# Later modulation loads queued behind the weights that the text loads ahead of them

## The chip, the core and the metric

The kernel runs on one core of a Trainium2 chip. A core has a matmul engine (TensorE, PE in the profile; its weight loads are PEld), VectorE (DVE), ScalarE (ACT), GpSimd (POOL) and SyncE (SP), which here issues every DMA. The engines run their own instruction lists in order and meet at semaphores. The metric is the device time of one execution in microseconds (us).

## The reference, cut to what matters

Two layers of a diffusion backbone work on 512 latent tokens and 256 context tokens of width 2048, all in float32. Each layer first computes a modulation from a conditioning vector, then norm, one input projection, two kinds of attention heads, a gate, and one output projection:

```python
mod = silu_c @ w_mod[l] + b_mod[l]                 # (1, 3 * 2048), context: silu_cc
shift, scale, gate = jnp.split(mod[:, None, :], 3, axis=-1)
h = rmsnorm(x, norm_g[l]) * (1.0 + scale) + shift
u = h @ e_w_in[i]                                  # even layer; o_w_in in the odd one
...                                                # heads, SiLU gate
x = x + gate * (y @ w_o[l])
```

Layer 0 (even) has eight differential heads (A) and eight windowed heads (B), layer 1 (odd) eight heads with normalised q and k (C) and eight latent heads (D). Context is updated by layer 0 alone. A final RMSNorm follows.

## The kernel before, in words

**Where the weights go.** Activations are kept transposed, 16 tiles of 128 channels by 768 tokens. A projection (`proj`, L313) makes 128 output channels: it loads a column of weights in two loads of 512 KB (`wraw`, L298, three buffers), splits each into a high and a low part (`wsplit`: ScalarE makes `wh` at L289, VectorE `wl` at L248, four buffers each of four k tiles), and runs three matmuls per k tile and token group (L308, L309, L311). I call the weight loads w1, w2, ... in the order in which the text makes them: 8 at the start, 8 per head of heads 1 to 7 of A (w9 to w64), 40 in B (w65 to w104), 32 in the output projection (w105 to w136), then those of layer 1.

**Where the modulation goes.** Scale and shift of layer 0 come first, by TensorE (`mod_first`, L142; 88 loads at the very start). The rest, called the later modulation, is `mod_later` (L173): the gate of layer 0, then scale and shift of layer 1, then the gate of layer 1, in sixteen blocks of 512 columns. A block takes eight loads of 512 KB (`mraw`, two buffers, L180). Each load is multiplied by the conditioning value of its row and added up in `macc` (one buffer): two k rows times two vectors (latent and context), so four operations of VectorE per load (L187; ScalarE does the first two of a block, L185). The gate of layer 1 needs one vector, so two. After eight loads VectorE transposes `macc` into the last `mraw` (L196) and reduces it into `parts` (L197, one buffer); after four blocks a small matmul with `fold` (L204) into a bank of the projections' pool adds the partitions up, and VectorE writes `modc` (L210). The 128 loads are called M1 to M128.

**What sets their place.** `later` (L229) is a generator that makes one load with its arithmetic at each step. The text calls `tick(n)` at fixed points, which adds n to a due count and makes as many steps as have come due: 0.4 after each projection of heads 1 to 7 of A, 3.5 after most projections of B, 2 after each of the sixteen chunks of the output projection of layer 0 (capped at 96 until layer 1 starts), 3.5 twice per head of C. That is the order of the text only. A scheduler that plays a timeline of the program orders each engine's list: an instruction that is ready goes ahead of an earlier one of the text that has to wait. TensorE's list is written by hand only for the start (L418). A block `tc.issue_after(ins)` adds an ordering edge without a semaphore: every instruction made inside it on the engine of `ins` stands behind `ins` in that engine's list. Before the change the loads of M1 to M96 stand behind `last_raw`, the last load of the first modulation, and M97 to M128 behind `last_x`, the last load of layer 1's activations; so a weight load that waits for a free `wraw` buffer lets any number of later-modulation loads pass that find a free `mraw` buffer.

**Who needs the results.** The gate of layer 0 and the scale of layer 1 are read in `out_chunk` (L707), the shift of layer 1 in `make_h` (L375) at the start of layer 1, the gate of layer 1 in the last output projection.

Of the kernel before, what the change touches and what calls it, by code (L numbers as in the profile page):

```python
# [17 lines left out]
P = 128  # L18
# [23 lines left out]
def trunk_kernel(ctx: ExitStack, tc: tile.TileContext, T):  # L42
    nc = tc.nc
# [84 lines left out]
    def mod_scale(dst, g0, nk, nv):  # L128
        nc.vector.scalar_tensor_tensor(dst, dst, 1.0, vcol[:, g0:g0 + nk].unsqueeze(2).broadcast_to([P, nk, nv]),
                                       op0=ALU.add, op1=ALU.mult)  # L130
# [7 lines left out]
            mod_scale(dst, V_NG + 16 * l + k0 - NCH, nk, nv)  # L138

    last_raw = [None]  # L140

    def mod_first(g):  # L142

        acc = pst.tile([P, 512], F32, name="T")
        for r0 in range(0, 32, 3):
            n = min(3, 32 - r0)

            i = r0 // 3
            if i < (11, 11, 11, 11, 11, 6, 4, 3)[g]:
                raw = hslot("mraw0", F32)  # L150
            elif g == 7 and i > 8:
                raw = wp.tile([P, 1024], F32, name="mraw", bufs=2)
            else:
                raw = slot("mraw0")
            last_raw[0] = nc.sync.dma_start(raw[:, :n * 256], T["wm0"][g][:, r0 * 256:(r0 + n) * 256])
            for i in range(n):
                sec, at = divmod(r0 + i, NCH)
                j = at % 4
                nc.tensor.matmul(acc[32 * j:32 * j + 32, 256 * sec:256 * sec + 256], lhsT=sil[:, at, :],
                                 rhs=raw[:, 256 * i:256 * i + 256], start=(at < 4), stop=(at >= NCH - 4),  # L160
                                 tile_position=(0, 32 * j))
            if r0 + n < 32:
                yield
        asb = sp["ep"].tile([P, TOK], F32, name="e")[:, 0:512]
        nc.scalar.copy(asb, acc)
        yield
        for i in range(4):
            nc.tensor.matmul(acc[:, 2 * i:2 * i + 2], lhsT=asb[:, P * i:P * i + P], rhs=sel, start=True, stop=True)
        for sec in range(2):
            mod_finish(0, 2 * g + NCH * (1 - sec), 2, acc[:, 4 * sec:4 * sec + 4].rearrange("p (c v) -> p c v", c=2))  # L170
        yield

    def mod_later(l, b, nv, behind=None):  # L173

        macc = sm.tile([P, 2, 512], F32, name="macc", bufs=1)
        for r in range(8):
            raw = wp.tile([P, 1024], F32, name="mraw", bufs=2)
            rv = raw.rearrange("p (k c) -> p k c", k=2)
            with tc.issue_after(behind.ins) if behind is not None else nullcontext():
                nc.sync.dma_start(raw, T["wm1"][b + 4 if l else b - 8, r])  # L180
            for i in range(2):
                for v in range(nv):
                    sc = silc[:, 16 * v + 2 * r + i:16 * v + 2 * r + i + 1]
                    if r == 0 and i == 0:
                        nc.scalar.mul(macc[:, v, :], rv[:, i, :], sc)  # L185
                    else:
                        nc.vector.scalar_tensor_tensor(macc[:, v, :], rv[:, i, :], sc, macc[:, v, :],  # L187
                                                       op0=ALU.mult, op1=ALU.add)
            if r < 7:
                yield  # L190

        if b % 4 == 0:
            parts[0] = sm.tile([P, 128], F32, name="parts", bufs=1)[:, :64 * nv].rearrange("p (b v c) -> p b v c", b=4, v=nv)
        part = parts[0][:, b % 4, :, :]
        turned = raw.rearrange("p (v c) -> p v c", v=2)[:, 0:nv, :]
        nc.vector.transpose(turned, macc[:, 0:nv, :])  # L196
        nc.vector.reduce_sum(part, turned.rearrange("p v (b c) -> p v b c", c=32), axis=AX.X)  # L197
        if b % 4 < 3:
            yield
            return  # L200


        mp = psj.tile([P, 512], F32, name="J")
        nc.tensor.matmul(mp[:, 0:64 * nv], lhsT=fold, rhs=parts[0].rearrange("p b v c -> p (b v c)"), start=True, stop=True)  # L204
        mv = mp[:, 0:64 * nv].rearrange("p (b v a c) -> p b a v c", b=4, v=nv, c=4)
        k0 = 4 * b - 12
        for c in range(4):
            rows = slice(32 * c, 32 * c + 32)
            bias = bmod[rows, 48 * l + k0:48 * l + k0 + 16].rearrange("p (b a) -> p b a", b=4)
            nc.vector.tensor_tensor(modc[l][rows, k0:k0 + 16, 0:nv].rearrange("p (b a) v -> p b a v", b=4),  # L210
                                    mv[rows, :, :, :, c], bias.unsqueeze(3).broadcast_to([32, 4, 4, nv]), op=ALU.add)
        if k0 == NCH:
            mod_scale(modc[l][:, k0:k0 + 16, :], V_NG + 16 * l, 16, nv)
        yield
# [14 lines left out]
    def later():  # L229
        for b in range(8, 12):  # L230
            yield from mod_later(0, b, 2, last_raw[0])
        for b in (4, 5, 6, 7, 0, 1, 2, 3):
            yield from mod_later(1, b, 2, last_raw[0])
        for b in range(8, 12):
            yield from mod_later(1, b, 1, last_x)
# [58 lines left out]
    def wraw(w, col, k0, nk, raw=None):  # L294

        if raw is None:
            raw = wp.tile([P, 1024], F32, name="wraw", bufs=3)
        nc.sync.dma_start(raw[:, :nk * P], w[col // P][:, k0 * P:(k0 + nk) * P])  # L298
        return raw[:, :nk * P].rearrange("p (k c) -> p k c", k=nk)

    def mm_step(lat, cx, wk, xk, first, last, opens=True, closes=True, at=(0, 512)):
# [11 lines left out]
    def proj(w, col, xs=None, lat_only=False, at=(0, 512)):  # L313
        xs = hT if xs is None else xs
        n = len(xs)
        lat = psj.tile([P, 512], F32, name="J")[:, :at[1] - at[0]]
        cx = None if lat_only else psj.tile([P, 512], F32, name="J")[:, :256]
        for k0 in range(0, n, 8):
            nk = min(8, n - k0)
            ws = wsplit(wraw(w, col, k0, nk), nk)  # L320
            for i in range(nk):
                mm_step(lat, cx, ws[i], xs[k0 + i], k0 + i == 0, k0 + i == n - 1, at=at)
        return lat, cx
# [71 lines left out]
    w = T["ew"]  # L395
# [10 lines left out]
    def start_loads(k):  # L406

        for i in range(4):
            raw = sm.tile([P, 2, 512], F32, name="macc", bufs=1).rearrange("p a b -> p (a b)") if i == 3 else None
            raws[i] = wraw(w, start_cols[i], k, 8, raw)  # L410
# [323 lines left out]
    for k in range(NCH):  # L734
        ys.append(load_y(0, k, TOK) if k < 14 else split(outs[k - 14], TOK, hslot, "y"))
        for j in range(2):
            if k % 8 == 0:
                ws4[j] = wsplit(wraw(wo, 128 * j, k, 8), 8)
            mm_step(two[j], two[2][:, 256 * j:256 * j + 256], ws4[j][k % 8], ys[k], k == 0, k == NCH - 1,
                    opens=(j == 0), closes=(j == 1))  # L740
# [7 lines left out]
    w = T["ow"]  # L748
# [346 lines left out]
```

## Time and profile before

| | |
|---|---|
| median of 3 runs | 2552.39 us (2547.49 to 2552.81) |
| profiled execution, time | 2551.65 us |
| profiled execution, span | 2549.9 us |
| TensorE busy | 2401.3 us, 94% |
| VectorE busy | 1609.5 us, 63% |
| ScalarE busy | 1012.1 us, 40% |
| read from HBM | 269.16 MB |
| mean granted TensorE clock | 0.979 |

The span runs from the first to the last instruction of the program. Busy times are unions of an engine's instructions. The views by stretch cut the span at given times and say for each engine how long it was busy there and how many instructions it ran; the granted clock is the share of full speed at which TensorE was let run. In the lists of waits an engine's idle time is put down to the instruction whose end released it. SyncE's own rows are the issues of DMAs. In time, the first modulation and the first projections take up to about 166 us, A lasts to about 910, B to about 1340, the output projection of layer 0 to about 1565; C ends near 2150, D near 2385, and the last output projection fills the rest.

### The profile page before, as it was taken

To read this page: it belongs to the slowest core of one execution; us is meant where nothing else is said; L and a number is where in the kernel's file an instruction comes from. 1 tells how busy PE (TensorE), PEld (TensorE's weight loads), DVE (VectorE), ACT (ScalarE), POOL (GpSimd) and SP (SyncE) were. 2 spreads that over 40 slices of the span, in tenths; PEclk is the share of its full clock that TensorE was granted. 3 is DMA by queue.
4 is the path that set the end of the run, shared out by engine and by line. 5 is a ranking of instruction groups with operands and counts; after the bars stand their busy time and mean duration, and the time that the engine had idled before them with its cause. 6 is when DMAs were issued, how large, how long until landed. Compare 5 with 4: busy or idle time off the path is not lost. (4 is left out here: it accounts for less than half of the span.)

```text
span 2549.9 us, 35926 instructions
## 1 busy us (share of the span) xinstructions
PE 2401.3 (94%) x14018; PEld 2063.7 (81%) x14018; DVE 1609.5 (63%) x2829; ACT 1012.1 (40%) x1964; POOL 252.8 (10%) x160
## 2 busy tenths in 40 slices
PE   3998898899999999999989999899999999999998
PEld 1677777788888898888888888678888888888787
DVE  4459999776556548976974333886535425776534
ACT  3234444355444434333352212434434434554434
POOL 1111001011000010010101111210010000100010
PEclk8999999899999999999999999999999999999999
DMA  8853443211111114532434334564222222122234
GB/s 307 304 173 121 135 133 119 76 48 56 56 57 58 57 56 130 175 114 98 165 121 141 118 128 149 183 213 133 76 74 79 71 91 71 62 87 71 95 116 149
DMA packets 97930, 297.44 MB, mean 117 GB/s; under 512 B 11489, under 2 KB 12513, under 8 KB 97761
## 3 DMA queue, kind: packets, MB, share of 16 engines
q1 hardware_dynamic: 97760, 295.16, 34.5%
q8 instruction: 110, 1.80, 0.3%
q14 instruction: 60, 0.48, 0.1%
HBM read 269.16 MB, written 25.95 MB: 116 GB/s over the span
## 5 line engine op out<-in xcount | busy, mean ns | idle before, releaser
L308 PE MATMUL J<-h,wh 128*128 128x512 f32 (+1 forms) x2224 | 794.9, 359 | 24.7 <-DVE sg L517 15.8
L309 PE MATMUL J<-l,wh 128*128 128x512 f32 (+1 forms) x2224 | 768.4, 354 | 2.5 <-DVE l L388 2.5
L311 PE MATMUL J<-h,wl 128*128 128x512 f32 (+1 forms) x2224 | 718.0, 356 | 11.1 <-DVE wl L248 11.1
L248 DVE TENSOR_TENSOR wl<-wraw,wh 128x512 fp32r<-128x512 f32 x500 | 361.3, 726 | 345.8 <-ACT wh L289 335.9
L289 ACT CAST wh<-wraw 128x512 fp32r<-128x512 f32 x492 | 303.4, 619 | 639.1 <-PE J L309 572.0
L308 PEld LDWEIGHTS J<-h,wh 128*128 128x128 f32 x2224 | 426.0, 192 | 109.2 <-DVE sg L517 17.1
L309 PEld LDWEIGHTS J<-l,wh 128*128 128x128 f32 x2224 | 426.6, 192 | 55.3 <-DVE l L388 3.2
L311 PEld LDWEIGHTS J<-h,wl 128*128 128x128 f32 x2224 | 395.0, 192 | 48.5 <-DVE wl L248 13.9
L187 DVE SCALAR_TENSOR_TENSOR macc<-mraw,silc,macc 128x512 f32<-128x512 f32 x420 | 324.6, 800 | 50.1 <-DMA mraw<-in_wm_dram 45.4
L308 PE MATMUL J<-yh,wh 128*128 128x512 f32 (+1 forms) x800 | 274.9, 350 | 3.3 <-ACT yh L493 2.7
L309 PE MATMUL J<-yl,wh 128*128 128x512 f32 (+1 forms) x800 | 272.2, 350 | 1.0 <-DVE yl L248 0.9
L311 PE MATMUL J<-yh,wl 128*128 128x512 f32 (+1 forms) x800 | 254.5, 349 | 0.0
L541 DVE TENSOR_REDUCE nb<-S 128x1 f32<-128x768 f32 (+3 forms) x208 | 165.8, 797 | 112.3 <-PE S L529 59.0
L576 ACT CAST pth<-T 128x256 fp32r<-128x256 f32 (+2 forms) x288 | 125.7, 451 | 191.5 <-PE T L572 188.3
L548 ACT ACTIVATE e<-S,nb 128x256 f32<-128x256 f32 (+3 forms) x144 | 104.3, 725 | 221.0 <-DVE nb L541 143.2
L248 DVE TENSOR_TENSOR ptl<-T,pth 128x256 fp32r<-128x256 f32 (+2 forms) x288 | 144.4, 513 | 59.5 <-ACT pth L576 57.3
L308 PEld LDWEIGHTS J<-yh,wh 128*128 128x128 f32 x800 | 149.9, 189 | 29.5 <-ACT yh L493 3.1
L309 PEld LDWEIGHTS J<-yl,wh 128*128 128x128 f32 x800 | 150.6, 189 | 22.1 <-DVE yl L248 2.9
L311 PEld LDWEIGHTS J<-yh,wl 128*128 128x128 f32 x800 | 140.7, 189 | 13.0
L455 POOL TENSOR_TENSOR r<-r,cos 128x512 f32<-128x512 f32 x31 | 45.6, 1471 | 842.6 <-DVE t L454 784.4
L572 PE MATMUL T<-identr,e 128*128 128x128 f32 x784 | 117.1, 275 | 11.6 <-DVE e L558 6.7
L572 PEld LDWEIGHTS T<-identr,e 128*128 128x128 f32 x784 | 94.1, 141 | 27.3 <-issue 5.5
(287 smaller groups left out, 3146.7 us busy)
## 6 DMA issues: line engine op xcount, KB each, us to landing
mraw<-in_wm_dram SPq DMA_DIRECT2D x128, 512.0 KB, 3.6
wraw<-in_ew_dram SPq DMA_DIRECT2D x102, 512.0 KB, 3.7
wraw<-in_ow_dram SPq DMA_DIRECT2D x64, 512.0 KB, 3.7
wraw<-in_wo_dram SPq DMA_DIRECT2D x62, 512.0 KB, 3.7
mraw<-in_wm_dram SPq DMA_DIRECT2D x80, 384.0 KB, 7.2
xT<-in_xT_dram SPq DMA_DIRECT2D x16, 384.0 KB, 7.8
res<-in_xT_dram SPq DMA_DIRECT2D x16, 384.0 KB, 4.3
xad<-nx SPq DMA_DIRECT2D x16, 384.0 KB, 2.4
```

Source lines behind the costliest of these rows:

```text
L187: nc.vector.scalar_tensor_tensor(macc[:, v, :], rv[:, i, :], sc, macc[:, v, :], op0=ALU.mult, op1=ALU.add)
L248: nc.vector.tensor_tensor(o, a, h.bitcast(F32), op=ALU.subtract)
L289: nc.scalar.copy(wh[:, :n, :], rv[:, k0:k0 + n, :])
L308: nc.tensor.matmul(o, lhsT=wh, rhs=xh[:, c0:c1], start=first and (opens or o is lat), stop=False)
L309: nc.tensor.matmul(o, lhsT=wh, rhs=xl[:, c0:c1], start=False, stop=False)
L311: nc.tensor.matmul(o, lhsT=wl, rhs=xh[:, c0:c1], start=False, stop=last and (closes or o is lat))
L455: nc.gpsimd.tensor_tensor(r[:, :512], r[:, :512], cos, op=ALU.mult)
L541: nc.vector.tensor_reduce(nb, S, axis=AX.X, op=ALU.max, negate=True)
L548: nc.scalar.activation(e, S, AF.Exp, bias=nb, scale=1.0 if scale is None else scale, accum_out=den)
L572: nc.tensor.transpose(out=tp[:, 128 * (b - b0):128 * (b - b0) + 128], in_=e[:, 128 * b:128 * b + 128], identity=ident)
L576: nc.scalar.copy(ph, tv)
```

## The change

A cell `last_w` remembers the latest weight load that `wraw` has made. Each load of the later modulation is put behind it in SyncE's list, in place of `last_raw` or `last_x`. The argument `behind` stays in the signature and is no longer used. No arithmetic, tile or buffer changes.

```diff
     last_raw = [None]
+    last_w = [None]
...
         for r in range(8):
             raw = wp.tile([P, 1024], F32, name="mraw", bufs=2)
             rv = raw.rearrange("p (k c) -> p k c", k=2)
-            with tc.issue_after(behind.ins) if behind is not None else nullcontext():
+
+            with tc.issue_after(last_w[0].ins):
                 nc.sync.dma_start(raw, T["wm1"][b + 4 if l else b - 8, r])
...
         if raw is None:
             raw = wp.tile([P, 1024], F32, name="wraw", bufs=3)
-        nc.sync.dma_start(raw[:, :nk * P], w[col // P][:, k0 * P:(k0 + nk) * P])
+        last_w[0] = nc.sync.dma_start(raw[:, :nk * P], w[col // P][:, k0 * P:(k0 + nk) * P])
         return raw[:, :nk * P].rearrange("p (k c) -> p k c", k=nk)
```

The loads of the latent heads' key weights (L893) do not go through `wraw` and are not remembered; no later-modulation load follows them.

## The prediction

> **What bounds the kernel now.** I read the page's head first, then a table by stretch of the span, then the same table for the accumulator of the later modulation alone, then TensorE's waits. The first two lines say that TensorE is the bound over the whole span.
>
> ```profile
> span 2549.9 us, 35926 instructions
> PE 2401.3 (94%) x14018; PEld 2063.7 (81%) x14018; DVE 1609.5 (63%) x2829; ACT 1012.1 (40%) x1964; POOL 252.8 (10%) x160
> ```
>
> The profiled execution has a span of 2549.9 us and a time of 2551.65 us; the sum below is made against the latter. The median of the runs is 2552.39, 0.74 above it. By stretch (columns: length, then busy us and count of PE, PEld, DVE, ACT, POOL, then granted clock, DMA share, GB/s):
>
> ```profile
> 166.00:540.00 374.00, 337.69 (x1939) 294.71 (x1934) 331.30 (x539) 163.31 (x306) 34.33 (x21) 0.95 0.36 114
> 540.00:803.00 263.00, 262.59 (x1622) 233.83 (x1621) 165.95 (x292) 124.98 (x239) 22.55 (x15) 1.00 0.16 53
> 803.00:910.00 107.00, 106.11 (x662) 94.63 (x661) 53.47 (x96) 46.15 (x89) 9.04 (x6) 1.00 0.17 54
> 910.00:972.00 62.00, 61.18 (x379) 54.67 (x378) 28.80 (x67) 22.77 (x56) 5.15 (x4) 1.00 0.18 61
> 972.00:1144.00 172.00, 171.17 (x1065) 153.44 (x1064) 159.60 (x294) 64.66 (x163) 21.17 (x12) 1.00 0.45 148
> 1144.00:1265.00 121.00, 115.12 (x693) 102.53 (x691) 95.58 (x183) 40.75 (x105) 10.94 (x7) 0.97 0.39 130
> 1265.00:1340.00 75.00, 62.37 (x400) 56.35 (x398) 57.02 (x128) 35.08 (x83) 3.03 (x2) 0.95 0.38 124
> 1340.00:1560.00 220.00, 219.10 (x1249) 191.83 (x1250) 79.62 (x111) 45.83 (x69) 25.16 (x13) 1.00 0.38 128
> 1600.00:1745.00 145.00, 127.91 (x610) 103.19 (x611) 125.34 (x184) 58.01 (x107) 27.29 (x14) 0.94 0.57 192
> 1745.00:2140.00 395.00, 394.10 (x2105) 338.98 (x2104) 172.66 (x307) 161.24 (x282) 31.48 (x23) 1.00 0.25 80
> ```
>
> From 540 to 972 and from 1745 to 2140 TensorE idles 3 us in all and has the full clock: nothing can be won there. What can be won is in 166 to 540 (36.3 us idle), in 1144 to 1340 (5.9 + 12.6) and in 1600 to 1745 (17.1). In each of these VectorE is busy for most of the time, and in each it works on the later modulation (the accumulator's instructions alone: length, DVE busy, ACT busy, clock, DMA):
>
> ```profile
> 166.00:540.00 374.00, 144.61 (x187) 8.02 (x12) 0.95 0.36 114
> 540.00:972.00 432.00, 0.00 (x0) 0.00 (x0) 1.00 0.17 55
> 972.00:1144.00 172.00, 91.96 (x119) 5.35 (x8) 1.00 0.45 148
> 1144.00:1265.00 121.00, 46.10 (x61) 2.68 (x4) 0.97 0.39 130
> 1265.00:1340.00 75.00, 7.54 (x7) 0.00 (x0) 0.95 0.38 124
> 1600.00:1745.00 145.00, 52.62 (x64) 2.89 (x4) 0.94 0.57 192
> ```
>
> Between 540 and 972 the accumulator has no instruction at all, and VectorE's own load in the even layer's heads is 165.95 of 263 us, 63%. In 166 to 540 the modulation adds 144.61 us, and what TensorE waits for there is mostly VectorE, or ScalarE work fed by it (us in total, times, longest):
>
> ```profile
> PE J L308 <- DVE sg L517: 10.8, 4, 4.3
> PE J L311 <- DVE wl L248: 9.2, 5, 5.0
> PE S L525 <- ACT e L548: 5.6, 3, 2.8
> ```
>
> The idle time is not all: after a stall the granted clock falls. One short stretch shows it best, 0.73 over 25 us, with the longest stall of that stretch 2.8 us:
>
> ```profile
> 370.00:395.00 25.00, 18.89 (x94) 16.79 (x95) 23.56 (x40) 9.36 (x18) 0.00 (x0) 0.73 0.36 107
> PE S L525 <- ACT e L548: 3.7, 2, 2.8
> ```
>
> Over 166 to 540 the mean is 0.95, so (1 - 0.95) x 374 = 18.7 us of full-clock work are lost as well. Idle and clock together make 36.3 + 18.7 = 55 us of that stage. In 1144 to 1340 it is 18.5 + 0.03 x 121 + 0.05 x 75 = 25.9 us, in 1600 to 1745 17.1 + 0.06 x 145 = 25.8 us.
>
> [...]
>
> **The change part by part.** Nothing is added or removed: the same 128 loads of 512 KB and the same arithmetic. What moves is where a load may stand in SyncE's queue. The order before (L180 are the later modulation's loads, L298 the weights'):
>
> ```profile
> L298 SPq DMA_DIRECT2D wraw<-in_ew_dram x9: 327/328/1488, 19.9 to 164.0; - x9
> L298 SPq DMA_DIRECT2D macc<-in_ew_dram x2: 327/573/819, 22.8 to 113.3; - x2
> L180 SPq DMA_DIRECT2D mraw<-in_wm_dram x48: 327/328/382, 166.2 to 474.4; - x48
> L298 SPq DMA_DIRECT2D wraw<-in_ew_dram x24: 327/328/382, 189.8 to 462.6; - x24
> L298 SPq DMA_DIRECT2D wraw<-in_ew_dram x46: 327/328/328, 491.9 to 970.4; - x46
> L180 SPq DMA_DIRECT2D mraw<-in_wm_dram x32: 327/328/779, 972.3 to 1143.9; - x32
> L298 SPq DMA_DIRECT2D wraw<-in_ew_dram x15: 327/328/328, 986.5 to 1135.3; - x15
> L180 SPq DMA_DIRECT2D mraw<-in_wm_dram x16: 327/328/328, 1194.8 to 1262.8; - x16
> L180 SPq DMA_DIRECT2D mraw<-in_wm_dram x32: 327/328/431, 1600.0 to 1732.2; - x32
> ```
>
> I number the weight loads w1, w2, ... and the modulation's M1 to M128. Eleven weight loads precede 166 us (the first row's 9, and the page's two into the accumulator's tile), so M1 to M48 stand between w11 and w36, M49 to M80 between w81 and w97, M81 to M96 behind w101 and ahead of w108, M97 to M128 in the odd layer's first 130 us. The text places them by its ticks: 28 ticks of 0.4 in the differential heads give 11 loads (M1 behind w14, M11 behind w64), 16 ticks of 3.5 in the windowed heads bring it to M67 (M12 behind w66, M32 behind w76, M64 to M67 behind w96), 2 per chunk of the output projection to M96 (M68 to M71 behind w108, M96 behind w134), and 3.5 twice per head of the odd layer (M97 to M103 behind w150, seven more every six weight loads). With the edge no load can stand ahead of these. So 37 loads leave the differential heads; the windowed heads get 56 by w97, where 32 stood, and the 16 behind w101 go; the output projection gets 29, where none were.
>
> Price of a load: 91.96 us / 32 = 2.9 us in 972 to 1144 and 144.61 / 48 = 3.0 in 166 to 540, plus an eighth of the reduction that the accumulator's rows leave out:
>
> ```profile
> L197 DVE TENSOR_REDUCE parts<-mraw x16: 668/1208/1220, 232.1 to 1739.8; 128x32 f32<-128x1024 f32 x12, 128x16 f32<-128x512 f32 x4
> ```
>
> 1.2 / 8 = 0.15, so 3.1 us of VectorE; in the odd layer (one vector, not two) 52.62 / 32 = 1.64, about 1.7.
>
> *Differential heads, 166 to 540.* TensorE's work at full clock is 337.7 - 18.7 = 319 us. VectorE's demand falls from 331.3 by 37 x 3.1 to about 217 us, 68% of 319, near the 63% at which 540 to 803 runs with 0.4 us idle. Not recovered are waits that do not come from the modulation: the start of the first head's chain and part of the softmax row of 5.6. I take 45 of the 55 us back; bounds 28 (half the idle and half the clock) and 52.
>
> *Windowed heads, 803 to 1144.* The weights' pace sets the loads' pace. The first row that matters is w66:
>
> ```profile
> 810.59 10.90 SPq L298 DMA_DIRECT2D wraw<-in_ew_dram  x2
> ```
>
> w66 goes at 810.6, w96 at 1135.3 (the row of 15), 30 loads in 325 us; 56 modulation loads by 3.1 us are 174 us, 53% of VectorE. Its own share is 53.47 / 107 = 50% in 803 to 910, 46% in 910 to 972, and (159.6 - 91.96 - 4.8) / 172 = 37% after that. So the sum is 103%, 99%, 90%: about full for 170 us. Of two rows it is between: 972 to 1144 ran with VectorE at 93% and 0.8 us idle; 166 to 540 had 89% and lost 55 of 374 us, 15%. By the first it costs 1 us, by the second 15% of the 169 us, 25 us. I take 9, nearer to the first, which has the same heads and weights; TensorE gets the weights early enough that some delay is hidden.
>
> *End of the windowed heads, 1144 to 1340.* M81 to M96 go away (46.1 + 7.5 us of VectorE), M57 to M71 come in part, M68 to M71 just where the last heads' softmax chain sets the pace. Of 25.9 us I take 5 back; bounds +6 and -15.
>
> *Output projection, 1340 to 1560.* 25 loads by 3.1 us add 78 us: VectorE goes from 79.6 to 157 of 220 us, 72%, and DMA from 128 GB/s by 13.1 MB / 220 us = 60. TensorE's need of VectorE is the evacuation of a bank per chunk and four weight splits, and a modulation operation ahead of these takes 0.8 us. I take +3; bounds 0 (its 93% row above) and 12 (half of what the odd layer's burst loses per load, below).
>
> *The fold's place.* The modulation's last use before the odd layer is a small matmul in TensorE's queue, in text order in both kernels:
>
> ```profile
> 969.39 0.38 PE L204 MATMUL J<-parts,fold 128*128 128x128 f32 x2
> 1564.04 0.38 PE L204 MATMUL J<-parts,fold 128*128 128x128 f32 x2
> ```
>
> M96 follows w134, and M97 to M103 follow w150:
>
> ```profile
> 1523.27 0.33 SPq L298 DMA_DIRECT2D wraw<-in_wo_dram  x1
> 1642.35 1.59 SPq L298 DMA_DIRECT2D wraw<-in_ow_dram  x2
> ```
>
> From 1523.3 to the matmul at 1564 there are 41 us for a last load, two accumulations, transpose and reduction (some 10 us), so the layer boundary gets no new wait; w76 against 969 leaves as much. If VectorE lagged by over 30 us there, TensorE would stand at the fold for the rest.
>
> *SyncE's queue.* A load waits for its buffer's last accumulation, and the next weight, the chunk's stores and the reads of y stand behind it:
>
> ```profile
> SPq L298 <- DVE wl L248: 1119.7, 219, 15.1
> SPq L180 <- DVE macc L187: 235.6, 77, 13.0
> ```
>
> 235.6 / 77 = 3 us per wait, against 5.1 us that a weight load itself waits for its buffer. As a weight goes out well ahead of its use (w134 above 41 us ahead of the fold that follows its chunk), 3 us are covered; without that cover 85 moved loads would show it, which is the third rival.
>
> *Odd layer's start, 1600 to 1745.* M97 starts at 1642 in place of 1600, and with w156 and w162 some 14 to 17 loads stand in the stretch in place of 32: VectorE falls from 125.3 to about 98 of 145 us, in the part where the new h tiles are made. I take 10 of 25.8 us back; bounds 0 and 20. What moves behind 1745 meets VectorE at 172.66 / 395 = 44%: nothing.
>
> Sum: -45 + 9 - 5 + 3 - 10 = -48 us; 2551.65 - 48 = 2503.65, and with the median's 0.74, 2504.
>
> **The rivals.** *The stalls come back in full.* VectorE falls below saturation everywhere: -52, +1, -15, 0, -20 make -86, so 2466. For it: 972 to 1144 at 93% without loss. Against: the odd layer's and the last heads' chains wait for ScalarE too.
>
> *Only half is kept.* The windowed heads behave as the differential heads did: +25 there, 12 in the projection, +6 at the end, against -45 and -10: -12, so 2540. For it: 100% of VectorE for 170 us. Against: the 93% row.
>
> *Each moved load blocks where it now stands: slower.* VectorE works in order, so an accumulation that waits for its load holds what stands behind it. The odd layer's burst shows the price: 25.8 us for 32 loads, 0.81 us each. The 56 + 29 loads would cost 85 x 0.81 = 69 us; less 45 and 10 that is +14, so 2566. It decides from 55 / 85 = 0.65 us per load. For it: the burst's DMA at 192 GB/s is what the output projection will have. Against: 972 to 1144 took 32 loads for under 1 us.
>
> *The change does not bring what it says.* The stalls of 166 to 540 belong to the first heads' own chain, and the loads were harmless: within 5 us of 2552. Against: the accumulator's 144.61 us lie in the saturated stretch and none in the clean one.
>
> **How the numbers follow.** Forecast 0.56, full return 0.12, half kept 0.16, blocked 0.12, nothing 0.04. What this kernel's measurement can tell from no change is about 0.2%, 5 us. Faster are the forecast, the full return and nearly all of the half (0.15 of 0.16), less 0.04 for the forecast's terms all at their bad ends (-28 + 25 + 6 + 12 + 0 = +15): 0.79. Within: 0.04 of the last rival, 0.01 of the half, 0.03 of that tail: 0.08. Slower: 0.12 and 0.01: 0.13. The range reaches down to the full return, 2466, and up to 2560, which takes in the half, nothing, and part of the blocked case; the forecast's own range is 2484 to 2524.
>
> **What would show each step.** The accumulator's busy time in 166 to about 740 should be some 35 us, and TensorE's idle time there under 10 us with a clock of 0.99 or more. The matmul that folds the first gate should come some 45 us earlier than 969. In the windowed heads VectorE should read 95% or more with TensorE's idle time under 10 us; in the output projection near 70%, with stalls behind the bank's evacuation of at most 0.3 us per chunk. The fold before the odd layer should have no wait ahead of it. The forecast is wrong if the first heads still stall behind their own chain, or if TensorE's waits for VectorE reappear in the windowed heads at 10% or more.

## The result and the profile after

The changed kernel takes 2518.82 us (median of 4 runs, 2515.45 to 2522.15), the kernel before 2551.85 (4 runs, 2547.49 to 2552.81). The ratio is 0.9874, 95% interval 0.9855 to 0.9893: 33 us, 1.3% faster, where the prediction had 48. The profiled execution of the changed kernel is its longest run, 2522.15 us; against the profiled one of before it is 29.5 us shorter. Its span is 2520.3 us.

In the changed kernel's text everything behind the cell `last_w` stands one or two lines lower: the fold is L206, the loads are L182, the accumulation L189. The table by stretch (same columns as before: length, PE, PEld, DVE, ACT, POOL, clock, DMA share, GB/s), cut where the same work starts and ends in this kernel:

```profile
166.00:520.00 354.00, 341.52 (x2069) 301.48 (x2068) 238.22 (x403) 167.88 (x317) 33.65 (x23) 0.99 0.18 61
520.00:762.00 242.00, 242.00 (x1494) 215.91 (x1493) 156.49 (x276) 115.39 (x221) 18.79 (x13) 1.00 0.19 64
762.00:929.00 167.00, 163.95 (x1009) 146.15 (x1007) 142.18 (x238) 65.88 (x130) 16.13 (x10) 1.00 0.42 140
929.00:1155.00 226.00, 219.00 (x1346) 195.21 (x1345) 190.82 (x369) 84.17 (x221) 23.85 (x14) 0.98 0.37 124
1230.00:1317.00 87.00, 69.61 (x388) 60.44 (x387) 66.94 (x149) 36.63 (x84) 0.00 (x0) 0.86 0.42 142
1317.00:1540.00 223.00, 222.67 (x1274) 195.15 (x1272) 140.81 (x198) 48.35 (x73) 24.84 (x13) 1.00 0.50 177
1575.00:1720.00 145.00, 133.46 (x654) 111.65 (x653) 107.18 (x161) 62.60 (x114) 27.55 (x14) 0.94 0.43 143
```

The stage that lost 55 us before now loses 12.5 us idle and about 3.5 us of clock, and 520 to 762 is clean. One stretch has become worse: 1230 to 1317, with 17.4 us idle and a granted clock of 0.86, against 12.6 and 0.95 in the rows of 1265 to 1340 before. The accumulator alone (length, DVE, ACT, clock, DMA):

```profile
166.00:520.00 354.00, 16.11 (x23) 1.95 (x3) 0.99 0.18 61
762.00:929.00 167.00, 70.45 (x94) 4.02 (x6) 1.00 0.42 140
1230.00:1317.00 87.00, 22.82 (x31) 1.34 (x2) 0.86 0.42 142
```

For a comparison stage by stage I use five marks that both kernels pass: the four folds of the later modulation on TensorE and the last windowed heads' output on VectorE. The first and third fold of before stand in the prediction; the other marks of before are

```profile
1191.28 0.38 PE L204 MATMUL J<-parts,fold 128*128 128x128 f32 x2
1339.54 0.49 DVE L670 SCALAR_TENSOR_TENSOR oB<-O,sg 128x128 f32<-128x128 f32 x2 [2.04 <-PE O L587]
1901.55 0.33 PE L204 MATMUL J<-parts,fold 128*128 128x64 f32 x2
```

and those of the changed kernel

```profile
928.87 0.38 PE L206 MATMUL J<-parts,fold 128*128 128x128 f32 x2
1154.54 0.38 PE L206 MATMUL J<-parts,fold 128*128 128x128 f32 x2
1315.38 0.49 DVE L672 SCALAR_TENSOR_TENSOR oB<-O,sg 128x128 f32<-128x128 f32 x2 [2.23 <-PE O L589]
1539.43 0.38 PE L206 MATMUL J<-parts,fold 128*128 128x128 f32 x2
1870.39 0.33 PE L206 MATMUL J<-parts,fold 128*128 128x64 f32 x2
```

Differences at the marks, after less before: -40.5 us at the first fold, -36.7 at the second, -24.2 at the last windowed output, -24.6 at the third fold, -31.2 at the fourth, -29.6 at the end of the span. So stage by stage: -40.5, +3.8, +12.6, -0.5, -6.5, +1.6. (The first fold lies inside the windowed heads, so the 40.5 holds their first part too, in which TensorE idles 3.1 us.) About 13 of the 37 us that are won at the second fold are given back by the end of the windowed heads. There the loads of the output projection start, behind w108:

```profile
1229.77 0.33 SPq L300 DMA_DIRECT2D wraw<-in_wo_dram  x1
1230.15 0.90 SPq L182 DMA_DIRECT2D mraw<-in_wm_dram  x2
1280.84 0.85 SPq L182 DMA_DIRECT2D mraw<-in_wm_dram  x2
```

M74 and M75 go out at 1280.8. VectorE's list just then, in order of time (the bracket is idle time before the instruction and what ended it):

```profile
1283.53 0.15 DVE L547 TENSOR_TENSOR nb<-nb,nsink 128x1 f32<-128x1 f32 x1
1286.08 1.41 DVE L189 SCALAR_TENSOR_TENSOR macc<-mraw,silc,macc 128x512 f32<-128x512 f32 x2 [2.41 <-DMA mraw<-in_wm_dram]
1287.41 0.15 DVE L554 TENSOR_TENSOR den<-den,es 128x1 f32<-128x1 f32 x1
1288.21 0.42 DVE L543 TENSOR_REDUCE nb<-S 128x1 f32<-128x256 f32 x1
1288.54 1.41 DVE L189 SCALAR_TENSOR_TENSOR macc<-mraw,silc,macc 128x512 f32<-128x512 f32 x2
1289.93 0.14 DVE L547 TENSOR_TENSOR nb<-nb,nsink 128x1 f32<-128x1 f32 x1
```

The softmax's `nb` at 1283.5 is done, but what follows it in the list is an accumulation that has to wait 2.4 us for its load; the next operation of the softmax chain (`den`) comes at 1287.4. The next scores are done at 1285.0 (the end of TensorE's last matmul before its wait), but VectorE takes their maximum (`nb`) only at 1288.2, and between its two `nb` operations stand two more accumulations. TensorE's longest wait of the stretch belongs to that chain:

```profile
PE S L527 <- ACT e L550: 7.9, 3, 5.7
```

The 5.7 us end at 1290.7. Of them, 1.1 are the rest of VectorE's wait for the load (1285.0 to 1286.1) and 2.8 are the four accumulations themselves (twice 1.41).

### The profile page after: what moved, and what is told of

The parts are those of the page before. It is cut to its first block, busy times and chain, and to the rows that moved or that the text cites. A ratio compares the mean times of both kernels' runs of the same rounds, so it can differ in the third digit from the quotient of the medians.

```text
span 2520.3 us, 35870 instructions
## 1 busy us (share of the span) xinstructions
PE 2394.1 (95%) x14018; PEld 2061.4 (82%) x14018; DVE 1607.8 (64%) x2829; ACT 1011.2 (40%) x1964; POOL 249.7 (10%) x160
## 4 chain that ended last, share of the span: by engine, by line
PE 80%; DVE 9%; DMA 6%; issue 2%; ACT 2%; SPq 0%; POOL 0%; ACTq 0%; DVEq 0%; POOLq 0%
PE J L310 20%; PE J L311 20%; PE J L313 20%; PE O L589 5%; DMA mraw<-in_wm_dram 5%; PE S L531 4%; PE T L574 3%; PE S L527 3%; DVE macc L189 2%; PE T L160 1%; DVE l L390 1%; DVE wl L250 1%; PE T L275 1%; PE T L255 1%; DVE nb L543 1%
## 5 line engine op out<-in xcount | busy, mean ns | idle before, releaser
L310 PE MATMUL J<-h,wh 128*128 128x512 f32 (+1 forms) x2224 | 789.9, 356 | 12.7 <-DVE vl L250 4.4
L313 PE MATMUL J<-h,wl 128*128 128x512 f32 (+1 forms) x2224 | 709.4, 354 | 2.2 <-DVE wl L250 2.2
L189 DVE SCALAR_TENSOR_TENSOR macc<-mraw,silc,macc 128x512 f32<-128x512 f32 x420 | 323.8, 804 | 79.7 <-DMA mraw<-in_wm_dram 68.7
L250 DVE TENSOR_TENSOR ptl<-T,pth 128x256 fp32r<-128x256 f32 (+2 forms) x288 | 144.5, 515 | 50.1 <-ACT pth L578 48.8
```

Source lines behind the costliest of these rows:

```text
L250: nc.vector.tensor_tensor(o, a, h.bitcast(F32), op=ALU.subtract)
L310: nc.tensor.matmul(o, lhsT=wh, rhs=xh[:, c0:c1], start=first and (opens or o is lat), stop=False)
L313: nc.tensor.matmul(o, lhsT=wl, rhs=xh[:, c0:c1], start=False, stop=last and (closes or o is lat))
```

## The experiments

All times are medians, and ratios are against runs of the kernel before on the same chip.

### Which part of the change brings what

Two kernels each with half the edge. The first:

```diff
-            with tc.issue_after(last_w[0].ins):
+            with tc.issue_after(last_w[0].ins if nv == 2 else behind.ins):
```

> The edge for M1 to M96 alone; M97 to M128 stay behind the last load of layer 1's activations. In the two traces the changed kernel gains 40.5 us up to the first fold and 6.5 us between the third and the fourth fold. If these are separate gains, this kernel keeps the first and loses the second: about 2519 + 6.5 = 2525 us, with the odd layer's first 145 us as before (TensorE idle about 17 us there). If the odd layer's gain came from the even layer's earlier end, it is within 2 us of 2519.

Measured: 2525.94 us, ratio 0.9900 (0.9884 to 0.9917). The second is the mirror image (`if nv == 1`):

> The edge for M97 to M128 alone; M1 to M96 stay behind the last load of the first modulation. Separate gains: the differential heads stay as before (span 166 to the first fold at 969 us, granted clock 0.95 in 166 to 540), and the whole is about 2552 - 6.5 = 2545 us. If the odd layer's start is bound by its own chain of norm and activations, it is within 2 us of 2552.

Measured: 2546.95 us, ratio 0.9990 (0.9980 to 0.9999). The two gains, 25 and 4 us, add up to 29 of the 33 us. The even layer's part stands by itself; the odd layer's is at the edge of what can be measured.

### The loads beside the last windowed heads

```diff
-        tick(2)
+        tick(2.7 if j > 3 else 0)
```

> The changed kernel, but the ticks of the output projection's first four chunks give nothing and the other chunks 2.7 each, so M68 stands behind w114 and not w108, and nothing of the later modulation runs while the last two windowed heads finish. Theory: the changed kernel lost 12 us there because accumulations that waited for their loads stood in VectorE's list ahead of the last heads' softmax (a stall of 5.7 us and a granted clock of 0.86 in 1230 to 1317). Then this stretch gets shorter by 8 to 15 us and the whole is 2504 to 2511 us. Rival: the last heads' chain is slow by itself as in the kernel before (13.4 us idle in 1255 to 1341), and this kernel is within 4 us of 2519.

Measured: 2517.12 us, ratio 0.9858 (0.9839 to 0.9877), the four runs from 2508.03 (the profiled one) to 2518.73. By the median that is the rival's number, but the trace shows the theory's gain and a second loss. Second fold and last windowed output:

```profile
1145.57 0.38 PE L206 MATMUL J<-parts,fold 128*128 128x128 f32 x2
1291.72 0.49 DVE L672 SCALAR_TENSOR_TENSOR oB<-O,sg 128x128 f32<-128x128 f32 x2 [2.23 <-PE O L589]
```

146.1 us between them, where the changed kernel has 160.8 and the kernel before 148.3: 15 us won back, as expected. (Nothing of the later modulation runs there now, so this takes away the accumulations and their waits together.) Then the two stretches, and in the second TensorE's and VectorE's waits:

```profile
1204.00:1293.00 89.00, 79.69 (x485) 69.30 (x483) 50.44 (x124) 37.58 (x88) 0.00 (x0) 0.98 0.34 108
1293.00:1529.00 236.00, 225.11 (x1274) 194.74 (x1274) 161.87 (x230) 49.20 (x75) 24.66 (x13) 1.00 0.53 185
```

```profile
PE J L310 <- DVE nx L713: 10.7, 8, 2.0
DVE macc L189 <- DMA mraw<-in_wm_dram: 32.3, 7, 5.3
```

From the last windowed output to the third fold the kernel before and the changed one take 224 us; here it is 237. With 2.7 loads per chunk, VectorE stands 32.3 us for loads in seven waits, up to 5.3 us each, and TensorE stands eight times behind the evacuation of a bank (`nx`). The loss had moved, not gone.

### VectorE's time or the loads

Three kernels made from the one before ask what the loss of 166 to 540 is made of. In the first, the second vector is not accumulated:

```diff
-                    else:
+                    elif v == 0:
                         nc.vector.scalar_tensor_tensor(macc[:, v, :], rv[:, i, :], sc, macc[:, v, :],
```

> The kernel before, without the accumulation of the second (context) vector in the later modulation: all 128 loads stay and stand as free as before, but a load costs VectorE half (the context's modulation is therefore left incomplete). Theory: in 166 to 540 VectorE was short of time, not the loads in the way; then the idle time of 36 us there falls under 12 us and the whole is about 2552 - 40 = 2512 us or lower. Rival: the loads hold the weights up in SyncE's queue or at the DMA engines; then the loads go out faster than before, the idle time stays at 30 us or more, and the whole stays above 2540 us.

Measured: 2533.79 us, ratio 0.9925 (0.9911 to 0.9940). Neither number came (the stretch, the accumulator alone, VectorE's waits for these loads):

```profile
166.00:540.00 374.00, 350.49 (x2067) 306.88 (x2067) 293.94 (x479) 172.36 (x325) 36.56 (x23) 0.97 0.35 115
166.00:540.00 374.00, 81.44 (x97) 8.02 (x12) 0.97 0.35 115
DVE macc L187 <- DMA mraw<-in_wm_dram: 18.0, 20, 3.6
```

23.5 us idle, clock 0.97. In the second the arithmetic is left out but for 32 columns:

```diff
-                    else:
-                        nc.vector.scalar_tensor_tensor(macc[:, v, :], rv[:, i, :], sc, macc[:, v, :],
+                    elif i == 1 and v == 0:
+                        nc.vector.scalar_tensor_tensor(macc[:, v, 0:32], rv[:, i, 0:32], sc, macc[:, v, 0:32],
```

> The kernel before with its loads as free as before, but all accumulation of the later modulation left out except one operation of 32 columns per load, which keeps each load in use (the later modulation is not computed). It tells VectorE's time from the loads. If VectorE's time is the cause, 166 to 540 has under 15 us idle, although 48 loads go out there faster than before, and the whole is 2490 to 2505 us. If loads ahead of the weights in SyncE's queue or at the DMA engines were the cause, the idle time is 25 us or more and the weights' casts wait for their data.

Measured: 2534.02 us, ratio 0.9941 (0.9926 to 0.9955). By stretch, then the accumulator alone, then VectorE's waits for these loads:

```profile
166.00:540.00 374.00, 351.14 (x2077) 307.64 (x2077) 239.98 (x439) 175.49 (x329) 34.70 (x23) 0.97 0.35 114
166.00:540.00 374.00, 20.87 (x54) 8.03 (x12) 0.97 0.35 114
DVE macc L187 <- DMA mraw<-in_wm_dram: 48.1, 31, 3.6
```

VectorE has 20.9 us of accumulation in place of 144.6, is busy for 64% of the stretch, and TensorE still idles 22.9 us. What remains of the accumulator is waiting: 31 times VectorE came to an accumulation whose load had not landed, 48.1 us in all. So my theory of VectorE's time falls as a full account; the rival as written (weights late) falls too, since no engine waits for a weight's load in this stretch. The loads also go out faster here: M48 at 325.0 and not at 474.4, and 21 of the 22.9 us idle stand before 300, with 39.4 of the 48.1 us of waits. A third account stands: a wait for a load inside VectorE's list holds up all that stands behind it. The counterpart keeps all arithmetic and takes the waits away:

```diff
         for r in range(8):
-            raw = wp.tile([P, 1024], F32, name="mraw", bufs=2)
-            rv = raw.rearrange("p (k c) -> p k c", k=2)
-            with tc.issue_after(behind.ins) if behind is not None else nullcontext():
-                nc.sync.dma_start(raw, T["wm1"][b + 4 if l else b - 8, r])
+            if r == 0:
+                raw = wp.tile([P, 1024], F32, name="mraw", bufs=2)
+                rv = raw.rearrange("p (k c) -> p k c", k=2)
+                with tc.issue_after(behind.ins) if behind is not None else nullcontext():
+                    nc.sync.dma_start(raw, T["wm1"][b + 4 if l else b - 8, r])
```

> The kernel before with all arithmetic of the later modulation, but one load per block of eight: the other seven rounds use the first load's data again (so the later modulation is computed from an eighth of its weights). It is the counterpart of the run without accumulation: VectorE's time without the waits for loads. There, 48 us of waiting for loads inside VectorE's list and hardly any arithmetic still lost 34 of 55 us in 166 to 540. If a wait inside VectorE's list holds TensorE up as operations do, and each us counts alike, this kernel (some 150 us of operations, few waits) still loses 40 to 55 us there and is 2535 to 2550 us. If the waits alone were the cause, it loses under 20 us there and is at 2515 us or below.

Measured: 2519.85 us, ratio 0.9884 (0.9868 to 0.9900): without the change's edge it is as fast as the changed kernel, and between the two forecasts. By stretch and the accumulator alone:

```profile
166.00:540.00 374.00, 349.61 (x2059) 305.15 (x2058) 338.61 (x553) 170.43 (x316) 36.16 (x23) 0.97 0.17 57
166.00:540.00 374.00, 144.52 (x187) 8.62 (x13) 0.97 0.17 57
```

and the waits for these loads in the same stretch of the kernel before:

```profile
DVE macc L187 <- DMA mraw<-in_wm_dram: 13.0, 8, 3.8
```

Idle plus clock over 166 to 540:

| kernel | accumulation, us | waits for loads, us | idle | (1 - clock) x 374 | lost |
|---|---|---|---|---|---|
| before | 144.6 | 13.0 | 36.3 | 18.7 | 55 |
| all arithmetic, one load per block | 144.5 | none listed | 24.4 | 11.2 | 36 |
| one vector | 81.4 | 18.0 | 23.5 | 11.2 | 35 |
| hardly any arithmetic | 20.9 | 48.1 | 22.9 | 11.2 | 34 |
| the changed kernel, 166 to 520 | 16.1 | 3.8 | 12.5 | 3.5 | 16 |

The last row is the same work with few of these loads: most of its 16 us belong neither to the accumulation nor to its waits. Both count: operations without waits add 20 us to it, waits with little work 18. But neither has a fixed price per us: taking 13 us of waits from a full VectorE gives 19 us back, so my expectation that each us counts alike was wrong. By which rule they combine is open. And the kernel with one load per block also has seven eighths less of these loads' traffic (57 GB/s in place of 114), so by itself it doesn't single out the waits; the second edge further down leaves the traffic as it is.

### Other ticks

Three kernels change the ticks alone (differential heads, windowed heads, output projection with nothing at its first four chunks). The diffs are of this form:

```diff
-        tick(.4 if h else 0)
+        tick(1.4 if h else 0)
...
-        tick(3.5)
+        tick(2.4)
...
-        tick(2)
+        tick(1.7 if j > 3 else 0)
```

> The changed kernel with other ticks: 1.4 in the differential heads (39 loads there), 2.4 in the windowed heads (to 77), nothing at the first four chunks of the output projection, 1.7 at the others. Theory: VectorE decides. With 39 loads its share in the differential heads is 63% + 39 x 3.1 / 590 = 83%, in the windowed heads about 85%, in the projection 36% + 1.7 x 3.1 / 16.8 = 67%; none is full, the last windowed heads have no load in their way and a chunk has fewer than the 2 that the changed kernel took without a stall. So the 13 us that the later start lost again at the chunks stay won: 2500 to 2509 us. Rival: the differential heads stall again as soon as loads come thicker than one per projection: 2515 us or more, with over 20 us idle before the first windowed head.

Measured: 2519.41 us, ratio 0.9885 (0.9871 to 0.9900): the rival. The differential heads, and VectorE's waits for these loads over the whole run:

```profile
166.00:768.00 602.00, 580.12 (x3505) 513.32 (x3504) 456.08 (x774) 283.53 (x535) 55.06 (x36) 0.99 0.25 83
DVE macc L189 <- DMA mraw<-in_wm_dram: 95.9, 57, 4.1
```

22 us idle in the differential heads with VectorE at 76%. The next has 0.7, 3.5 and 1.9:

> The changed kernel with 0.7 per tick in the differential heads (20 loads), 3.5 in the windowed heads as before (to 76), nothing at the first four chunks of the output projection, 1.9 at the others. Theory: below 2 loads per chunk the evacuation of a bank is not held up (no stall of TensorE behind it over 0.5 us), the last heads gain as with the later start, and the windowed heads are as in the changed kernel: 2504 to 2511 us. Rival: what stalled the chunks was that loads run into the last chunks at all, then about 2517 us as with the later start.

Measured: 2512.16 us, ratio 0.9859 (0.9842 to 0.9877), 1 us above the theory's range. One stall of 0.6 us behind a bank is left in the projection, where the theory allowed 0.5. VectorE's waits over the whole run:

```profile
DVE macc L189 <- DMA mraw<-in_wm_dram: 80.2, 53, 3.9
```

The last has 1.8, 2.9 and none:

> The changed kernel with 1.8 per tick in the differential heads (50 loads) and 2.9 in the windowed heads (to 96), none in the output projection. VectorE's share: 63% + 50 x 3.1 / 590 = 89% and about 94%. If only a full VectorE costs anything, this gives 2500 to 2510 us. If stalls set in well below that, in proportion to the modulation's share (the kernel before lost 55 us for 48 loads in 166 to 540), it is 2520 us or more, and the spread with 39 and 38 loads is better by 10 us.

Measured: 2524.55 us, ratio 0.9904 (0.9882 to 0.9926). So stalls set in well below a full VectorE, and the thicker the loads stand in the differential heads the more there are.

### The waits by themselves

If waits inside VectorE's list are what is left, they can be taken out without touching the work: a second edge puts a load's accumulations behind the last weight split that the text makes ahead of them. Weights precede the load in SyncE's list, so by the time their split is done the load should have landed.

```diff
+    last_s = [None]
...
-                        nc.vector.scalar_tensor_tensor(macc[:, v, :], rv[:, i, :], sc, macc[:, v, :],
-                                                       op0=ALU.mult, op1=ALU.add)
+                        with tc.issue_after(last_s[0].ins):
+                            nc.vector.scalar_tensor_tensor(macc[:, v, :], rv[:, i, :], sc, macc[:, v, :],
+                                                           op0=ALU.mult, op1=ALU.add)
...
-            sub(wl[:, :n, :], rv[:, k0:k0 + n, :], wh[:, :n, :])
+            last_s[0] = sub(wl[:, :n, :], rv[:, k0:k0 + n, :], wh[:, :n, :])
```

(`sub` returns its instruction.) The waits to be removed, over the whole run, in the kernel before and in the changed one:

```profile
DVE macc L187 <- DMA mraw<-in_wm_dram: 45.4, 31, 3.9
```

```profile
DVE macc L189 <- DMA mraw<-in_wm_dram: 68.7, 48, 5.2
```

The change had raised them from 45.4 to 68.7 us. My reading is that a load behind a weight lands later than the plan of VectorE's list has it. The trace shows the waits and the landing (the median from issue to landing of these loads went from 3.6 to 4.6 us), not the plan. With the second edge on the changed kernel:

> The changed kernel with a second edge, on VectorE: the accumulations of a load stand behind the last weight split that the text makes ahead of them, so the load has long landed when VectorE comes to them. VectorE's operations are the same; its waits for these loads (20 us in 762 to 1155, 6 in 1155 to 1317, 20 in 1317 to 1540) should fall below 10 us in all. Theory: these waits stand ahead of the softmax and of the bank's evacuation; without them the last windowed heads lose their 5.7 us stall, and the whole is 2500 to 2512 us. Rival: a buffer is now held until the split, some 20 us; with two buffers SyncE stands at the next load with the weights behind it, the splits come late, and the whole is 2520 us or more.

Measured: 2513.31 us, ratio 0.9855 (0.9842 to 0.9869), 1.3 us above the theory's range. Windowed heads, last windowed heads, and the waits over the whole run:

```profile
762.00:1155.00 393.00, 387.32 (x2385) 345.61 (x2384) 343.78 (x617) 152.08 (x355) 41.67 (x24) 1.00 0.40 132
1155.00:1310.00 155.00, 141.15 (x866) 124.11 (x866) 92.38 (x210) 62.07 (x150) 9.31 (x6) 0.99 0.31 106
DVE macc L191 <- DMA mraw<-in_wm_dram: 14.3, 11, 4.1
```

The waits are down from 68.7 to 14.3 us, the 5.7 us stall is gone, and the clock of the last heads is 0.99, where the changed kernel has 0.93 over 1155 to 1317. In the windowed heads the edge takes away the waits alone: 173.1 us of accumulation in 762 to 1155, against 166.3 in the changed kernel, and TensorE's idle time falls from 10.1 to 5.7 us. In the last windowed heads it also moves work: between the second fold and the last windowed output stand 16 accumulations and not 31, so there it does not tell waits from work. On the kernel with 0.7, 3.5 and 1.9:

> The same second edge on the kernel with 0.7, 3.5, and 1.9 from the fifth chunk (2512 us). If waits for loads are what is left, 2498 to 2506 us; if the buffers' being held costs more where 3.5 loads go with two weight loads, 2515 us or more.

Measured: 2497.52 us, ratio 0.9797 (0.9784 to 0.9810), half a us below its range. The waits:

```profile
DVE macc L191 <- DMA mraw<-in_wm_dram: 13.7, 11, 3.4
```

On the kernel with 1.4, 2.4 and 1.7:

> The same second edge on the kernel with 1.4, 2.4, and 1.7 from the fifth chunk (2519 us, with 32 us of VectorE waiting for these loads in the differential heads and 22 us of TensorE idle there). With the edge these waits go, and with fewer loads per weight load two buffers suffice: 2495 to 2505 us, the idle time in the differential heads under 12 us. If VectorE's operations alone stall the differential heads, it stays at 2515 us or more.

Measured: 2501.43 us, ratio 0.9810 (0.9796 to 0.9823):

```profile
DVE macc L191 <- DMA mraw<-in_wm_dram: 13.3, 10, 3.1
166.00:760.00 594.00, 576.68 (x3491) 511.75 (x3492) 456.23 (x768) 283.79 (x535) 58.98 (x36) 0.99 0.25 84
755.00:1230.00 475.00, 473.58 (x2944) 424.28 (x2942) 352.79 (x644) 184.72 (x434) 51.25 (x30) 1.00 0.32 105
```

18 us faster than the same ticks without the edge, with 83 us less of waiting (95.9 to 13.3). The windowed heads have 1.4 us idle in 475. The differential heads still have 17 us idle in 594, where the same ticks without the edge had 22 in 602, not under 12: most of TensorE's stalls there do not come from these waits, and there the rival was right. That two buffers would be too few, the rival of the first two, came true in neither.

The kernel with 0.7, 3.5, 1.9 and the second edge is the fastest of this study: 52 us less than the kernel before on the same chip, about 20 less than the changed one.

## Why the prediction was right or wrong

The direction, the places of the loads among the weights (to within a few weights) and the time's range were right; the size was 15 us too large by the medians and 18.4 by the traces. Point by point, as predicted and as measured at the marks:

| step | predicted, us | measured, us |
|---|---|---|
| differential heads | -45 | -40.5 (to the first fold) |
| windowed heads | +9 | +3.8 (first to second fold) |
| end of the windowed heads | -5 (bounds +6 and -15) | +12.6 |
| output projection | +3 | -0.5 |
| odd layer's start | -10 | -6.5 |
| rest | 0 | +1.6 |

*Differential heads.* Right. The accumulator fell from 144.6 us to 16.1 in 166 to 520, the clock rose to 0.99, the fold came 40.5 us earlier, and the half with the even layer's edge alone shows that it belongs to this part. TensorE's idle time, 12.5 us up to 520, stayed above the 10 that the prediction named as a sign. The reason given was too narrow: the prediction took VectorE's operations as the cause, and the runs show operations and waits for loads inside VectorE's list side by side, 20 and 18 us above what the changed kernel still loses when each stands nearly alone.

*Windowed heads.* The sum of 103% of VectorE did not come about. The weights kept nearly the pace forecast (w66 at 772.2, w96 at 1106.8, 335 us where the sum had 325). M12 to M67 go out and are added up in

```profile
772.00:1126.00 354.00, 343.95 (x2117) 306.48 (x2116) 306.08 (x551) 135.69 (x316) 37.39 (x22) 0.99 0.41 138
```

Here the instructions on `mraw` take 170.0 us of VectorE, 48% and not 53%, and all that is not theirs takes 38%, where the sum had 50, 46 and 37. Together VectorE was at 86%, and the stage cost 4 us.

*End of the windowed heads.* This is the step that failed, and it failed outside its bounds: its 17.6 us are nearly all of the 18.4 that are missing. That the other misses, of 2 to 5 us each, cancel is luck. The prediction saw that M68 to M71 would stand where the last heads' softmax sets the pace, and priced it as a part of the load that left. But eight loads stood there, M68 to M75, and each cost far more than it allowed. From the second fold to the last windowed output:

| kernel | length, us | accumulations beside the last softmax | VectorE's waits for loads, us | TensorE idle, us | clock |
|---|---|---|---|---|---|
| before | 148.3 | 7 | 2.0 | 12.6 | 0.98 |
| changed | 160.8 | 31 | 6.1 | 16.2 | 0.93 |
| later start | 146.1 | 0 | none | 8.1 | 0.99 |
| second edge on the changed kernel | 152.9 | 16 | none | 12.7 | 0.99 |

The kernels with half the edge repeat the first two lengths: 160.7 us with the even layer's edge, 148.2 with the odd layer's. Against before, the changed kernel loses 3.6 us by idle time and (1 - 0.93) x 160.8 - (1 - 0.98) x 148.3 = 8.3 us by the clock. The kernel before has 62 accumulations in this stage, but 55 of them run ahead of 1265, where the last heads' softmax begins. So the lengths follow the accumulations beside the softmax, and not their number in the stage; how much of the price is the accumulations' own time and how much their waits stays open, since both go down together in these runs (in the 5.7 us stall they are 2.8 and 1.1 us). That loads would block where they stand was on paper as the third rival, with 0.81 us for each of 85 moved loads; it came true at one place only. The later start moved M68 to M75 away and won 14.7 / 8 = 1.8 us per load back. In the windowed heads and the projection VectorE waits for these loads as well (some 20 us each, the numbers in the expectation above), and there the stages lost 4 us and nothing.

*Output projection and the folds.* Right: 2 loads per chunk fit, no stall behind a bank, 140.8 of 223 us busy (63%, predicted 72: 21 loads were left for it and not 25), and the fold before the odd layer had no wait. The run with 2.7 loads per chunk shows how near the edge that was.

*Odd layer's start.* Right in sign, 3.5 us too large; the half with the odd layer's edge alone gives 4 us.

*The clock.* The prediction counted lost clock beside idle time, by the granted clock of the rows, and the runs bear that out. In the changed kernel's 1230 to 1317 it is (1 - 0.86) x 87 = 12 us. The stall of 5.7 us is followed by the first row below, (1 - 0.51) x 14 = 6.9 us; no other stall of the stretch is over 2.4 us, and they have the other 5 us. Single stalls far from others cost clock too: in the kernel before, the second row follows a stall of 3.0 us, and the last stall over 0.4 us before that one lies more than 50 us back.

```profile
1288.00:1302.00 14.00, 10.27 (x41) 9.16 (x42) 10.57 (x32) 3.68 (x12) 0.00 (x0) 0.51 0.00 0
271.00:274.00 3.00, 3.00 (x16) 3.00 (x15) 3.00 (x6) 1.84 (x3) 0.00 (x0) 0.50 0.00 0
```

The run with 2.7 loads per chunk shows the other side: eight stalls of at most 2.0 us, some 18 us apart, left the clock at 1.00.

## What to carry to other kernels

Before moving a background load, look at where its consumer stands in its engine's list: a consumer that comes before its data is a wait for all that follows, and it shows up as another engine's slowness (here TensorE's stalls behind VectorE were put down to softmax and weight splits, and taking 83 us of VectorE's waits for background loads away made one kernel 18 us faster). Order both ends: the load behind the weights that are urgent, and the arithmetic behind something that is sure to come after the landing. And don't spread background work by the engine's share alone; where a serial chain sets the pace, such as the last heads' softmax, eight loads cost 12.6 us, and the 21 in the output projection nothing that these profiles show.

## What the runs showed that I had not expected

A kernel with 144.5 us of accumulation and no waits and one with 20.9 us of it and 48.1 us of waits lost the same 34 to 36 us of TensorE, of which the changed kernel still loses 16. Small stalls can cost clock beside idle time (one of 3.0 us, followed by a clock of 0.50 for 3 us), or none (eight of up to 2.0 us at 1.00); what tells the two apart is open. And one program's runs differ by more than 10 us without any difference in the program: the later start gave 2508.03 to 2518.73 us, the odd layer's edge alone 2543.24 to 2555.55, and the second fold, up to which the kernel of the later start has the changed one's text, came 9 us earlier in its profile, so stage differences of a few us between two profiled executions carry no weight unless another kernel repeats them.
